# A hybrid transformer block on one core: both seams of its feed-forward rebuilt

## The chip, the cores and the metric

The kernel runs on one core of a Trainium2 chip. The metric is device time in microseconds (us) of one execution, from runs of the kernel before and of the changed one on the same chip. The engines are PE (TensorE, the matrix engine), DVE (VectorE), ACT (ScalarE), POOL (GpSimd) and SP (SyncE, which here only issues DMA transfers). Each runs its own instructions in a fixed order; they wait for each other through semaphores.

## The reference

One residual block on x of 1024 rows (tokens) by 1024 columns: a mixing layer, a cross-attention, and the feed-forward part that the change is about. All in fp32.

```python
D_MODEL, SEQ, D_FF = 1024, 1024, 2816
def reference(x, mem, ...):
    ...
    h = h + jnp.concatenate([ret, fox], axis=-1) @ w_out[l]
    h = h + memory_cross_attention(rmsnorm(h, g_xattn[l]), mem, ...)
    hn = rmsnorm(h, g_ffn[l])
    h = h + (jax.nn.silu(hn @ w_gate[l]) * (hn @ w_up[l])) @ w_down[l]
    return h
```

## The kernel before

**Precision.** PE multiplies fp32 values as pairs: a high part (ACT casts it to a rounded format: `act.copy(hi, x)`) and a low part (DVE: `lo = x - hi`). A product is three matmuls, hi·hi, hi·lo and lo·hi (`into`, L1153 to L1160, per block of 128 in the contraction). So each operand costs an ACT cast and a DVE subtraction before PE can use it.

**Stages.** They run one after the other (`whole`): mixing, cross-attention, its output projection (`xo_main`, which also normalises h for the feed-forward: `f_norm(t)` for the eight row tiles t of 128), the hidden stage (`hidden_main`) and the down stage (`down_main`). The places where the hidden stage starts and ends are the two seams.

**Hidden stage.** The 1024x1024 normalised input is taken as 2x2 blocks x11, x12 (row tiles 0 to 3, tile `xr0`) and x21, x22 (row tiles 4 to 7, `xr1`), and for each of 22 chunks f of 128 hidden columns the weights of gate and up as a second 2x2 matrix. Seven block products in the manner of Strassen and Winograd, P1, Q5, P6, P2, P7, Q3, Q4 (`step`), take the place of eight; each has 12 matmuls of 128x512. On the input side that needs four sums of blocks, s1 = x21 − x22, s3 = x11 − x21, s2 = s1 − x11, s4 = x12 + s2; on the weight side t13 (two sums), t2, t4 per chunk (`weights_of`). P1 and P2 need x11 and x12 alone, so those of the first three chunks run before the first seam (AHEAD = 3). After them, once all eight `f_norm` are done, the four sums and the five split operands are made on whole 128x2048 tiles (L1233 to L1254). Weights come by four loads per chunk into `raw_w` (two buffers, `load_w`), POOL makes the sums, ACT and DVE split them, up to eight products ahead of PE. The result of a chunk, 128x1024, is built in `at` (one buffer) and stored to `a_dram` by SP (L1222).

**Down stage.** Strassen's seven products again, over groups of chunks: GROUPS are four groups of 6, 6, 6 and 4 chunks, each split in two halves along the contraction. Per group eight blocks are loaded (A11 to A22 from `a_dram`, B11 to B22 from w_down; `load`, ten buffers `raw_d`), POOL makes eight combinations into `st` (`combine`), ACT and DVE split 14 operands into `op` tiles (12 buffers), PE runs 7 products x 4 row tiles, and DVE adds each 128x512 result onto the output rows `hh0` to `hh7`, which are loaded from `h_dram` (L1388) and stored to `out` in the last group. Operands are made up to three products ahead.

**Order.** PE's order is written out by hand (`manual_schedule`); on the other engines a scheduler sets it, and a tile's memory may be taken by a later tile once the readers of the first are done, across `pool`s too. So a load can wait for work on quite other data whose memory it takes over. `sp.dma_start` puts a transfer on SP's queue, `pol.dma_start` on POOL's.

Of the kernel before, what the change touches and what calls it, by code (L numbers as in the profile page):

```python
# [1455 lines left out]
```

## Time and profile before

| | us |
|---|---|
| three runs | 1649.39, 1650.70, 1653.69; median 1650.7 |
| profiled execution | 1651.59, of which the span of the core 1649.7 |
| PE busy | 1558.5 (94% of the span) |
| DVE busy | 959.0 (58%) |
| ACT busy | 753.6 (46%) |
| POOL busy | 390.9 (24%) |

Busy time is a sum over the whole span; the stages differ. How to read it: the chain of waits tells which engine's work set the end, a table of stretches tells where that engine stood still or had a lower clock (PEclk, as a share of full speed), and the timeline of such a stretch tells what it waited for, in brackets behind the first instruction after a pause. A row's duration includes a little of the instruction's start and end, so rows of one engine overlap slightly. The end of a matmul in the trace is modelled; the distance from start to start is what counts.

### The profile page before, as it was taken

The numbers are of one execution on the slowest core, as the hardware profiler recorded it, in microseconds if no ns is written. First come the engines' busy times: TensorE is split into PE (matmuls) and PEld (weight loads), VectorE is DVE, ScalarE is ACT, GpSimd is POOL, SyncE is SP. The second block draws the span as 40 slices with busy tenths as digits, with TensorE's granted clock in tenths as the row PEclk, the third lists the DMA queues.
The fourth block names the chain that finished last, engine by engine and source line by source line (L and its number), as shares of the span: only waits on it lengthen the run. The fifth ranks groups of instructions, "written<-read, shape, count | busy, mean of one in ns | idle before, by whom it ended". The sixth has DMA issues, their size and how long they took to land.

```text
span 1649.7 us, 22047 instructions
## 1 busy us (share of the span) xinstructions
PE 1558.5 (94%) x7960; PEld 1313.2 (80%) x7960; DVE 959.0 (58%) x1984; ACT 753.6 (46%) x1630; POOL 390.9 (24%) x387
## 2 busy tenths in 40 slices
PE   7999999999999999999899929999999999589999
PEld 7997898898887878888788817888888887468887
DVE  6667657657668832655644365443444442788877
ACT  5456656656568820555634433333333332323332
POOL 0332232232231000000000033223222220757541
PEclk9999999999999999999999969999999999789999
DMA  7021111121133461202523023222222211833202
GB/s 222 18 75 46 44 52 46 37 60 46 35 114 122 146 205 39 65 14 64 154 83 109 39 76 102 90 77 77 78 90 88 78 51 45 324 123 107 89 15 103
DMA packets 142927, 142.16 MB, mean 86 GB/s; under 512 B 9177, under 2 KB 110809, under 8 KB 142306
## 3 DMA queue, kind: packets, MB, share of 16 engines
q1 hardware_dynamic: 142818, 140.75, 27.1%
q8 instruction: 63, 1.03, 0.3%
q14 instruction: 46, 0.38, 0.1%
HBM read 112.38 MB, written 28.34 MB: 85 GB/s over the span
## 4 chain that ended last, share of the span: by engine, by line
PE 81%; DVE 6%; ACT 5%; DMA 3%; issue 2%; POOL 2%; SPq 0%; POOLq 0%; DVEq 0%; ACTq 0%
PE ps_mm L270 10%; PE ps_mm L271 10%; PE ps_mm L272 10%; PE ps_s L1157 6%; PE ps_s L1158 6%; PE ps_s L1159 6%; PE ps_tp L175 5%; PE ps_tp L1157 3%; PE ps_tp L1159 3%; PE ps_tp L1158 3%; PE ps_mm L1159 2%; PE ps_mm L1158 2%; PE ps_mm L1157 2%; PE ps_s L270 1%; PE ps_pv L696 1%
## 5 line engine op out<-in xcount | busy, mean ns | idle before, releaser
L270 PE MATMUL ps_mm<-w_hi,cv_hi 128*128 128x512 f32 x384 | 155.4, 405 | 6.9 <-DVE h L838 3.5
L272 PE MATMUL ps_mm<-w_hi,cv_lo 128*128 128x512 f32 x384 | 152.1, 396 | 0.0
L271 PE MATMUL ps_mm<-w_lo,cv_hi 128*128 128x512 f32 x384 | 151.7, 395 | 0.0
L1292 ACT CAST w_hi<-t 128x512 fp32r<-128x512 f32 x88 | 54.4, 620 | 171.3 <-PE ps_tp L1158 72.6
L1293 DVE TENSOR_TENSOR w_lo<-t,w_hi 128x512 fp32r<-128x512 f32 x88 | 65.1, 742 | 83.3 <-ACT w_hi L1292 83.2
L1278 POOL TENSOR_TENSOR t<-raw_w 128x1024 f32<-128x1024 f32 x22 | 53.2, 2417 | 250.8 <-DVE w_lo L1293 227.8
L240 DVE TENSOR_TENSOR w_lo<-raw,w_hi 128x1024 fp32r<-128x1024 f32 (+2 forms) x75 | 88.2, 1181 | 30.3 <-ACT w_hi L239 29.3
L239 ACT CAST w_hi<-raw 128x1024 fp32r<-128x1024 f32 (+2 forms) x75 | 74.9, 1003 | 59.2 <-PE ps_mm L272 39.9
L1247 POOL TENSOR_TENSOR xr<-xr,xr 128x2048 f32<-128x2048 f32 x1 | 4.5, 4550 | 396.7 <-DVE s L1245 396.7
L270 PE MATMUL ps_mm<-w_hi,hn_last 128*128 128x384 f32 (+2 forms) x256 | 96.3, 376 | 1.0 <-DVE t L291 1.0
L270 PE MATMUL ps_mm<-w_hi,hn_hi 128*128 128x384 f32 (+2 forms) x256 | 96.4, 377 | 0.1
L271 PE MATMUL ps_mm<-w_lo,hn_hi 128*128 128x384 f32 (+2 forms) x256 | 91.4, 357 | 0.0
L272 PE MATMUL ps_mm<-w_hi,hn_lo 128*128 128x384 f32 (+2 forms) x256 | 91.1, 356 | 0.0
L270 PEld LDWEIGHTS ps_mm<-w_hi,cv_hi 128*128 128x128 f32 x384 | 73.0, 190 | 22.4 <-DVE h L838 4.0
L272 PE MATMUL ps_mm<-w_hi,hn_last 128*128 128x384 f32 (+2 forms) x256 | 90.1, 352 | 0.0
L271 PE MATMUL ps_mm<-w_lo,hn_last 128*128 128x384 f32 (+2 forms) x256 | 89.8, 351 | 0.0
L1337 DVE TENSOR_TENSOR op<-st,op 128x1536 fp32r<-128x1536 f32 (+1 forms) x32 | 79.9, 2530 | 11.8 <-ACT op L1336 11.8
L272 PEld LDWEIGHTS ps_mm<-w_hi,cv_lo 128*128 128x128 f32 x384 | 72.8, 190 | 16.9
L1293 DVE TENSOR_TENSOR w_lo<-raw_w,w_hi 128x512 fp32r<-128x512 f32 x60 | 46.3, 771 | 67.4 <-ACT w_hi L1292 67.4
L271 PEld LDWEIGHTS ps_mm<-w_lo,cv_hi 128*128 128x128 f32 x384 | 73.0, 190 | 14.7
L1336 ACT CAST op<-st 128x1536 fp32r<-128x1536 f32 (+1 forms) x32 | 43.0, 1372 | 86.2 <-POOL st L1332 30.6
L1332 POOL TENSOR_TENSOR st<-raw_d 128x1536 f32<-128x1536 f32 (+1 forms) x16 | 63.9, 4004 | 66.4 <-DMA raw_d<-a_dram 56.7
(394 smaller groups left out, 4577.5 us busy)
## 6 DMA issues: line engine op xcount, KB each, us to landing
raw_w<-w_gate SPq DMA_DIRECT2D x44, 256.0 KB, 3.8
raw_w<-w_up SPq DMA_DIRECT2D x44, 256.0 KB, 4.2
a_dram<-at SPq DMA_DIRECT2D x22, 512.0 KB, 2.6
raw_d<-a_dram SPq DMA_DIRECT2D x12, 768.0 KB, 6.5
raw_d<-w_down SPq DMA_DIRECT2D x12, 768.0 KB, 6.3
raw<-w_in SPq DMA_DIRECT2D x32, 256.0 KB, 4.2
raw<-w_xkv SPq DMA_DIRECT2D x16, 512.0 KB, 3.8
of<-o_dram SPq DMA_DIRECT2D x16, 512.0 KB, 4.1
```

Of the source, the lines that this page charges most:

```text
L175: flip = lambda o, x: mm.transpose(o, x, ident)
L239: act.copy(hi, raw)
L240: dve.tensor_tensor(lo, raw, f32(hi), ALU.subtract)
L270: mm.matmul(o, xh, wh, start=first, stop=False)
L271: mm.matmul(o, xh, wl, start=False, stop=False)
L272: mm.matmul(o, xl, wh, start=False, stop=last)
L1157: mm.matmul(q, wh, xh, start=first and k == 0, stop=False, skip_group_check=True)
L1158: mm.matmul(q, wh, xl, start=False, stop=False, skip_group_check=True)
L1159: mm.matmul(q, wl, xh, start=False, stop=k == n - 1, skip_group_check=True)
L1293: dve.tensor_tensor(lo, x, f32(hi), ALU.subtract)
L1332: pol.tensor_tensor(t, x, y, op)
L1337: dve.tensor_tensor(lo, x, f32(hi), ALU.subtract)
```

## The change

**First seam.** The tiles of h become pairs, so that the first pair can be read as one 128x4x512 tile (`h01`). For t from 4 on, `f_norm` makes the four sums for its 128 rows on DVE, s1 into `h01`, the others in place in `xr`. Behind the seam only the five splits are left, in two slices of columns, 384 and 128. The rows of h are stored to `h_dram` from POOL's queue. The weight tiles `raw_w`, t13, t2 and t4 get a pool of their own (`ra`), and the three weight sums move from POOL to DVE.

**Second seam.** `a_dram` is stored from POOL's queue. The ten `raw_d` buffers are named slots; the first three lie in a pool (`down_r0`) where `ra` was. Three groups of 6, 8 and 8 chunks take the place of four; a buffer holds up to four chunks. The combinations are made on DVE, in place in `raw_d`, and `op` has 10 buffers. Loads are issued as slots come free, up to one group ahead.

```diff
-    GROUPS = [[list(range(f, f + n)), list(range(f + n, f + 2 * n))] for f, n in ((0, 3), (6, 3), (12, 3), (18, 2))]
+    GROUPS = [[list(range(f, f + n)), list(range(f + n, f + 2 * n))] for f, n in ((0, 3), (6, 4), (14, 4))]
...
-        h = [hp.tile([P, D], F32, name=f"h{t}") for t in range(NT)]
-        st["h"] = h
+        pairs = [hp.tile([P, 2, D], F32, name=f"h{t}") for t in range(NT // 2)]
+        st["h"] = [pairs[t // 2][:, t % 2] for t in range(NT)]
+        st["h01"] = pairs[0].rearrange("p a (b c) -> p (a b) c", c=512)
...
-            sp.dma_start(h_dram[t], h[t])
+            pol.dma_start(h_dram[t], h[t])
...
+            if t >= 4:
+                x11, x12, x21, x22 = (st["xr"][i // 2][:, 4 * (i % 2):4 * (i % 2) + 4, cols] for i in range(4))
+                s1 = st["h01"][:, :, cols]
+                dve.tensor_tensor(s1, x21, x22, ALU.subtract)
+                dve.tensor_tensor(x21, x11, x21, ALU.subtract)
+                dve.tensor_tensor(x11, s1, x11, ALU.subtract)
+                dve.tensor_tensor(x12, x12, x11, ALU.add)
...
-                            sp.dma_start(a_dram[g][i][fs.index(f)], c)
+                            pol.dma_start(a_dram[g][i][fs.index(f)], c)
...
-        s12 = pool("ffn_s", 1, stack=tmp).tile([P, 4, 512], F32, name="s12")
-        dve.tensor_tensor(s12, x21, x22, ALU.subtract)
-        A["Q5"] = operand("s1", s12)
-        pol.tensor_tensor(x21, x11, x21, ALU.subtract)
...
+        xs = {"Q5": st["h01"], "P6": xr[0][:, :4], "P7": xr[1][:, :4], "Q3": xr[0][:, 4:], "Q4": xr[1][:, 4:]}
+        for what, x in xs.items():
+            A[what] = [wp[0].tile([P, 4, 512], F32R, name=f"x{what}{i}") for i in range(2)]
+        for cols in (slice(0, 384), slice(384, 512)):
+            for what, x in xs.items():
+                hi, lo = (y[:, :, cols] for y in A[what])
+                act.copy(hi, x[:, :, cols])
+                dve.tensor_tensor(lo, x[:, :, cols], f32(hi), ALU.subtract)
...
+        ra = pool("ffn_a", 1, side="right", stack=RR)
...
-            raw[f] = r = rr.tile([P, 4, 4, P], F32, name="raw_w", tag="raw_w", bufs=2)
+            raw[f] = r = ra.tile([P, 4, 4, P], F32, name="raw_w", tag="raw_w", bufs=2)
...
-                pol.tensor_tensor(t13[f], r[:, 0:2], r[:, 1:3], ALU.add)
+                dve.tensor_tensor(t13[f], r[:, 0:2], r[:, 1:3], ALU.add)
...
-            x = dr.tile([P, 3, 512], F32, name="raw_d", tag="raw_d", bufs=10)[:, :len(fs)]
+            i = room.pop(0)
+            x = dr[i // 3 > 0].tile([P, 4, 512], F32, name="raw_d", tag=f"raw_d{i}")[:, :len(fs)]
...
-            pol.tensor_tensor(t, x, y, op)
...
+            elif what == "Q5":
+                sub(a11, a11, a21)
+                sub(a21, a21, a22)
+                add(b11, b11, b12)
+                x, y = a21, b11
+            elif what == "P6":
+                dve.scalar_tensor_tensor(a21, a11, -1.0, a22, ALU.mult, ALU.subtract)
+                add(b11, b11, b22)
+                x, y = a21, b11
...
+            while todo and room and todo[0][0] <= g + 1:
+                load(*todo.pop(0))
```

DVE's order at the first seam, before (`xr_10132` is `xr0` with x11 and x12, `xr_10133` is `xr1` with x21 and x22, `s_10759` the buffer of s1 and s2):

```order
L1190 TENSOR_TENSOR p_10693<-ps_mm,p_10693 128x512
L1245 TENSOR_TENSOR s_10759<-xr_10133 128x2048
L1190 TENSOR_TENSOR p_10734<-ps_mm,p_10734 128x512
L1239 TENSOR_TENSOR s1l<-s_10759,s1h 128x2048
L1239 TENSOR_TENSOR s3l<-xr_10133,s3h 128x2048
L1248 TENSOR_TENSOR s_10759<-s_10759,xr_10132 128x2048
L1239 TENSOR_TENSOR x22l<-xr_10133,x22h 128x2048
L1239 TENSOR_TENSOR s2l<-s_10759,s2h 128x2048
L1250 TENSOR_TENSOR xr_10132<-xr_10132,s_10759 128x2048
L1239 TENSOR_TENSOR s4l<-xr_10132,s4h 128x2048
L1293 TENSOR_TENSOR w_lo<-t_10803,w_hi 128x512
```

and now (`xr_10126` and `xr_10127` are `xr0` and `xr1`, `h_7710` the pair `h01`, `t_10817` the weight sum t13; L1200 is the addition behind P2):

```order
L1125 TENSOR_TENSOR h_7710<-xr_10127 128x4x128
L1126 TENSOR_TENSOR xr_10127<-xr_10126,xr_10127 128x4x128
L1127 TENSOR_TENSOR xr_10126<-h_7710,xr_10126 128x4x128
L1128 TENSOR_TENSOR xr_10126<-xr_10126 128x4x128
L1200 TENSOR_TENSOR p_10744<-ps_mm,p_10744 128x512
L1251 TENSOR_TENSOR xQ_10767<-h_7710,xQ_10766 128x4x384
L1251 TENSOR_TENSOR xP_10769<-xr_10126,xP_10768 128x4x384
L1251 TENSOR_TENSOR xP_10771<-xr_10127,xP_10770 128x4x384
L1251 TENSOR_TENSOR xQ_10773<-xr_10126,xQ_10772 128x4x384
L1251 TENSOR_TENSOR xQ_10775<-xr_10127,xQ_10774 128x4x384
L1251 TENSOR_TENSOR xQ_10767<-h_7710,xQ_10766 128x4x128
L1251 TENSOR_TENSOR xP_10769<-xr_10126,xP_10768 128x4x128
```

The sums stand ahead of the last P2's addition (L1200) now, the low parts (L1251) behind it in slices, and the first weight sum, which was POOL's, follows them on DVE after five of 128 columns.

SP's queue at the second seam, before:

```order
L1222 DMA a_dram_1_74<-at 128x1024
L1325 DMA raw_d<-a_dram_0_67 128x3x512
L1222 DMA a_dram_1_74<-at 128x1024
L1327 DMA raw_d<-w_down 128x3x512
L1325 DMA raw_d<-a_dram_0_67 128x3x512
L1325 DMA raw_d<-a_dram_1_68 128x3x512
L1327 DMA raw_d<-w_down 128x3x512 x2
L1325 DMA raw_d<-a_dram_1_68 128x3x512
L1327 DMA raw_d<-w_down 128x3x512
L1325 DMA raw_d<-a_dram_0_69 128x3x512
L1327 DMA raw_d<-w_down 128x3x512
L1388 DMA hh_13876<-h_dram 128x1024
```

and now:

```order
L1270 DMA raw_w<-w_gate 128x4x128
L1325 DMA raw_d<-a_dram_0_67 128x3x512
L1327 DMA raw_d<-w_down 128x3x512
L1325 DMA raw_d<-a_dram_0_67 128x3x512
L1385 DMA hh_13891<-h_dram 128x1024
L1385 DMA hh_13893<-h_dram 128x1024
L1385 DMA hh_13895<-h_dram 128x1024
L1325 DMA raw_d<-a_dram_1_68 128x3x512
L1327 DMA raw_d<-w_down 128x3x512 x2
L1325 DMA raw_d<-a_dram_1_68 128x3x512
L1327 DMA raw_d<-w_down 128x3x512
```

The store of `a_dram` is no longer on this queue; A11, B11 and A21 come right behind the last weights, three of the `hh` loads follow, and the fourth load (A22, `a_dram_1_68`) heads the rest.

DVE's order at the second seam, before (`st` are POOL's combinations, `op` the split operands):

```order
L1218 TENSOR_TENSOR at<-at,s_13802 128x512
L1337 TENSOR_TENSOR op_13841<-raw_d,op_13840 128x1536
L1337 TENSOR_TENSOR op_13845<-raw_d,op_13844 128x1536
L1337 TENSOR_TENSOR op_13853<-st,op_13852 128x1536
L1337 TENSOR_TENSOR op_13857<-st,op_13856 128x1536
L1337 TENSOR_TENSOR op_13869<-st,op_13868 128x1536
L1337 TENSOR_TENSOR op_13873<-st,op_13872 128x1536
L1337 TENSOR_TENSOR op_13935<-st,op_13934 128x1536
L1337 TENSOR_TENSOR op_13939<-raw_d,op_13938 128x1536
L1400 TENSOR_TENSOR hh_13876<-hh_13876,ps_s 128x512
```

and now:

```order
L1228 TENSOR_TENSOR at<-at,s_13816 128x512
L1333 TENSOR_TENSOR op_13859<-raw_d,op_13858 128x1536
L1333 TENSOR_TENSOR op_13863<-raw_d,op_13862 128x1536
L1343 TENSOR_TENSOR raw_d<-raw_d 128x1536
L1397 TENSOR_TENSOR hh_13891<-hh_13891,ps_s 128x512
L1343 TENSOR_TENSOR raw_d<-raw_d 128x1536
L1397 TENSOR_TENSOR hh_13893<-hh_13893,ps_s 128x512
L1342 TENSOR_TENSOR raw_d<-raw_d 128x1536
L1333 TENSOR_TENSOR op_13874<-raw_d,op_13873 128x1536
L1333 TENSOR_TENSOR op_13878<-raw_d,op_13877 128x1536
L1353 SCALAR_TENSOR_TENSOR raw_d<-raw_d 128x1536
L1342 TENSOR_TENSOR raw_d<-raw_d 128x1536
```

The combinations (L1342, L1343, L1353) stand in DVE's order between the low parts, and two of the output rows (L1397) stand ahead of the sums that need A22 and B12.

## Rows read from the trace of the kernel before

**Rows 1.** the page's part 4, shares of the chain of waits by engine.

```profile
PE 81%; DVE 6%; ACT 5%; DMA 3%; issue 2%; POOL 2%; SPq 0%; POOLq 0%; DVEq 0%; ACTq 0%
```

**Rows 2.** stretches: us, busy us by engine, PEclk, DMA share, GB/s.

```profile
900.00:949.30 49.30, 49.24 (x230) 40.17 (x228) 18.79 (x32) 18.34 (x32) 1.67 (x1) 1.00 0.09 33
949.30:988.00 38.70, 7.69 (x25) 5.42 (x25) 24.73 (x16) 13.39 (x16) 12.31 (x7) 0.65 0.30 82
988.00:1050.00 62.00, 61.07 (x253) 48.71 (x254) 32.42 (x42) 21.24 (x38) 22.39 (x13) 0.97 0.31 95
1050.00:1401.00 351.00, 351.00 (x1500) 282.15 (x1498) 137.73 (x205) 118.26 (x205) 84.89 (x48) 1.00 0.24 74
1401.00:1457.00 56.00, 30.94 (x93) 22.45 (x92) 43.16 (x15) 15.14 (x11) 43.90 (x10) 0.73 0.77 281
1520.00:1649.70 129.70, 126.06 (x557) 104.04 (x555) 102.93 (x104) 37.78 (x31) 50.93 (x15) 1.00 0.21 72
```

**Rows 3.** timeline, PE: start, us, line, op, out<-in, count, [idle <-releaser].

```profile
978.27 0.80 PE L1157 MATMUL ps_tp<-s1h,w_hi 128*128 128x512 f32 x1 [29.04 <-ACT w_hi L1292]
...
982.93 0.40 PE L1157 MATMUL ps_s<-s2h,w_hi 128*128 128x512 f32 x1
...
987.92 0.50 PE L1157 MATMUL ps_tp<-s4h,w_hi 128*128 128x512 f32 x1 [2.02 <-ACT q L1197]
```

**Rows 4.** timeline, DVE, first seam.

```profile
945.26 2.29 DVE L1245 TENSOR_TENSOR s<-xr 128x2048 f32<-128x2048 f32 x1 [1.66 <-ACT xr L1113]
...
949.95 4.38 DVE L1239 TENSOR_TENSOR s1l<-s,s1h 128x2048 fp32r<-128x2048 f32 x1
...
954.25 2.28 DVE L1239 TENSOR_TENSOR s3l<-xr,s3h 128x2048 fp32r<-128x2048 f32 x1
...
967.30 2.29 DVE L1239 TENSOR_TENSOR s4l<-xr,s4h 128x2048 fp32r<-128x2048 f32 x1 [1.96 <-ACT s4h L1238]
```

**Rows 5.** timeline, ACT, SP's queue and POOL, first seam.

```profile
944.17 1.06 ACT L1113 COPY xr<-ps_tp 128x512 f32<-128x512 f32 x2
...
969.74 0.38 SPq L1272 DMA_DIRECT2D raw_w<-w_gate  x1
...
975.23 2.34 POOL L1278 TENSOR_TENSOR t<-raw_w 128x1024 f32<-128x1024 f32 x1 [23.05 <-DMA raw_w<-w_up]
...
977.60 0.62 ACT L1292 CAST w_hi<-t 128x512 fp32r<-128x512 f32 x1 [10.33 <-POOL t L1278]
```

**Rows 6.** timeline, PE, second seam.

```profile
1410.03 0.80 PE L1157 MATMUL ps_s<-op,op 128*128 128x512 f32 x1 [8.68 <-ACT op L1336]
...
1421.55 0.50 PE L1157 MATMUL ps_mm<-op,op 128*128 128x512 f32 x1
...
1426.55 0.80 PE L1158 MATMUL ps_mm<-op,op 128*128 128x512 f32 x1 [4.50 <-DVE op L1337]
...
1446.97 0.77 PE L1157 MATMUL ps_s<-op,op 128*128 128x512 f32 x1 [9.52 <-DVE hh L1400]
```

**Rows 7.** timeline, SP's queue, DVE, ACT and POOL, second seam.

```profile
1402.80 0.32 SPq L1222 DMA_DIRECT2D a_dram<-at  x1
...
1403.44 1.76 DVE L1337 TENSOR_TENSOR op<-raw_d,op 128x1536 fp32r<-128x1536 f32 x1 [0.67 <-ACT op L1336]
...
1408.51 1.47 ACT L1336 CAST op<-raw_d 128x1536 fp32r<-128x1536 f32 x1 [5.10 <-DMA raw_d<-w_down]
...
1413.03 6.95 POOL L1332 TENSOR_TENSOR st<-raw_d 128x1536 f32<-128x1536 f32 x2 [56.71 <-DMA raw_d<-a_dram]
...
1414.18 12.37 SPq L1388 DMA_DIRECT2D hh<-h_dram  x8
...
1441.26 4.97 DVE L1337 TENSOR_TENSOR op<-raw_d,op 128x1536 fp32r<-128x1536 f32 x1
```

**Rows 8.** groups by form, DVE, 1050 to 1649: busy us, mean ns | idle.

```profile
L1400 DVE TENSOR_TENSOR hh<-hh,ps_s 128x512 f32<-128x512 f32 x42 | 27.2, 679 | 4.2 <-PE ps_s L1159 4.2
```

**Rows 9.** the page's part 6, DMA issues: count, KB each, median us to landing.

```profile
a_dram<-at SPq DMA_DIRECT2D x22, 512.0 KB, 2.6
```

More of the change, by code (lines that the diff above doesn't have):

```diff
@@ L1314, in down_main @@
         dl = pool("down_l", 1)
-        dr = pool("down_r", 1, side="right")
-        raw, tmp = {}, {}
+        dr = [pool(f"down_r{i}", 1, side="right") for i in range(2)]
+        BLOCKS = ("A11", "B11", "A21", "A22", "B12", "B22", "A12", "B21")
+        raw = {}
+        room = list(range(10))
         def load(g, name):
@@ L1338, in split @@
             return hi, lo
-        LOADS = {"P1": ("A11", "B11"), "Q5": ("A21", "A22", "B12"), "P6": ("B22",), "Q3": ("A12",), "P2": ("B21",)}
         PRODUCTS = ("P1", "Q5", "P6", "Q3", "P7", "P2", "Q4")
+        todo = [(g, x) for g in range(len(GROUPS)) for x in BLOCKS]
         def operands(g, what):
-            r = lambda name: raw[g, name]
-            t = lambda name: tmp[g, name]
+            a11, b11, a21, a22, b12, b22, a12, b21 = (raw[g, x][0] for x in BLOCKS)
+            add = lambda o, x, y: dve.tensor_tensor(o, x, y, ALU.add)
+            sub = lambda o, x, y: dve.tensor_tensor(o, x, y, ALU.subtract)
@@ L1356, in operands @@
-            if what == "Q3":
-                combine(g, "S4", r("A12"), t("S2"), ALU.add)
-                return split(t("S4")) + split(r("B22"))
-            if what == "P7":
-                combine(g, "S3", r("A11"), r("A21"), ALU.subtract)
-                combine(g, "T3", r("B12"), r("B22"), ALU.add)
-                return split(t("S3")) + split(t("T3"))
-            if what == "P2":
-                return split(r("A12")) + split(r("B21"))
-            combine(g, "T4", t("T2"), r("B21"), ALU.add)
@@ L1366, in operands @@
-            return split(r("A22")) + split(t("T4"))
+                x, y = a11, b11
+            elif what == "Q5":
[7 more added lines that the diff above has]
+                x, y = a21, b11
+            elif what == "Q3":
+                add(a21, a21, a12)
+                x, y = a21, b22
+            elif what == "P7":
+                add(b12, b12, b22)
+                x, y = a11, b12
+            elif what == "P2":
+                x, y = a12, b21
+            else:
+                add(b11, b11, b21)
+                x, y = a22, b11
@@ L1368, in down_main @@
+            made = split(x) + split(y)
+            for name in {"Q3": ("A21",), "P7": ("A11", "B12", "B22"), "P2": ("A12",), "Q4": ("B21", "A22", "B11")}.get(what, ()):
+                room.append(raw[g, name][1])
+            while todo and room and todo[0][0] <= g + 1:
+                load(*todo.pop(0))
+            return made
         banks = [[ps_s(), ps_s(), ps_s(), ps_pv()], [ps_mm(), ps_mm()] + [ps_tp().rearrange("p a b -> p (a b)") for _ in range(2)]]
         seq = [(g, p) for g in range(len(GROUPS)) for p in PRODUCTS]
-        loads = [(g, x) for g, p in seq for x in LOADS.get(p, ())]
@@ L1371, in down_main @@
-        for x in loads[:8]:
-            load(*x)
-        loaded = 8
+        for _ in BLOCKS:
+            load(*todo.pop(0))
         made = []
@@ L1376, in down_main @@
             while len(made) < min(n + 3, len(seq)):
[L1377 to L1384 removed]
+                made.append(operands(*seq[len(made)]))
             if n == 0:
```

49 lines of the change are left out of this document (8 added, 41 removed).

## The prediction

> **What bounds the kernel now.** I read the page's chain of waits first, then a table of stretches, then the timeline of the two stretches in which the matrix engine is not full. The chain belongs to PE for 81% [rows 1], so only time that PE stands still, or runs at its lower clock, can be won. The table [rows 2] shows where that is: from 900 to 949.3 us PE is busy 49.24 of 49.30, from 1050 to 1401 all of 351.00. The holes are 949.3 to 988 (7.69 of 38.70, granted clock 0.65) with some remainder up to 1050, and 1401 to 1457 (30.94 of 56.00, granted clock 0.73). A matmul of the hidden stage takes 351.00/1500 = 0.234 us, of the down stage 126.06/557 = 0.2263. So the first seam loses 38.70 + 62.00 − (25 + 253) × 0.234 = 35.6 us, the second 56.00 − 93 × 0.2263 = 35.0 us. These 70.6 us are all that the change can touch; it leaves the number of matmuls (924 in the down stage either way) as it was.
>
> In the first seam PE waits 29.04 us for the first w_hi [rows 3]. The chain behind it: DVE makes the sums and low parts from 945.26 one after the other, until 967.30 + 2.29 = 969.6 [rows 4]; only then does SP issue the first raw_w load (969.74), because its buffer lies where the operands' inputs were; POOL starts the sum of weights when it has landed (975.23), ACT casts at 977.60 [rows 5]. The matmuls then start at half speed: Q5's twelve take 982.93 − 978.27 = 4.66 us, where 12 × 0.234 = 2.81, and another 2.02 us wait follows for ACT's copy q [rows 3].
>
> In the second seam PE waits 8.68 us for ACT's cast of B11 [rows 6], which came by a load that SP issues right behind the stage's last store (1402.80 + 0.32, so at about 1403.2), 5.3 us before the cast at 1408.51 [rows 7]. Then 4.50 us for a low part and 9.52 us for DVE's output rows [rows 6]: POOL makes the combinations one after another from 1413.03, and DVE runs beside it at 4.97 us for a tile that took 1.76 alone [rows 7].
>
> **First seam, part by part.** The four sums move ahead of the seam: per row tile t from 4 to 7, four DVE operations of 128x4x128, each about a 128x512 one, 0.68 us [rows 8]; taken at 0.60 where they follow each other (a row's end lies 0.08 behind the next one's start: 949.95 + 4.38 against 954.25 [rows 4]). 16 × 0.60 = 9.6 us go into a stretch where DVE is busy 18.79 of 49.30 [rows 2]: hidden, and at PE's cost only if DVE lacked 20 us more there. The last tile's copies end at 944.17 + 1.06 = 945.23 [rows 5], so its sums are done at 945.26 + 4 × 0.60 = 947.7, before PE's last matmul ends (978.27 − 29.04 = 949.23).
>
> What is left behind the seam: ten casts on ACT, and ten low parts on DVE (five of 1536 columns, five of 512). ACT starts at about 947.0 and needs 5 × 1.40 + 5 × 0.52 = 9.6 us; it stays ahead. DVE is free after the last P2 eviction at 949.95, where s1l starts before [rows 4]. The five large ones at 1.67 (1.76 less the overlap [rows 7]) end at 958.3, the small ones at 0.60 at 961.3. The sum of weights t13, now on DVE (1024 columns, 2 × 0.60 less one overhead, 1.13), ends at 962.4; ACT's cast of 0.62 [rows 5] lets PE start at about 963.15. Loads of raw_w now wait for h stores only, long landed, so they cover themselves; without that cover they would add 5.5 us (969.74 to 975.23).
>
> PE starts 978.27 − 963.15 = 15.1 us earlier. The 2.02 wait, and the half-clock stretch behind it, go as well: by my order of ACT, q is copied at 970.0 and P6 ends at 963.15 + 4.66 + 2.81 = 970.6. Lost after: 963.15 − 949.23 = 13.9, and 4.66 − 2.81 = 1.85 for the clock; 15.75 in place of 35.6. **Gain 19.9 us.** POOL's sums of weights go to DVE in the hidden stage too: 22 chunks × (1.13 + 0.60 + 0.60) = 2.3 us per chunk, where DVE is busy 137.73 of 351 us, 7.7 per chunk of 19.7 [rows 2]. 10.0 of 19.7 stays hidden; in return DVE's low parts no longer run beside POOL.
>
> **Second seam.** A11, B11 and A21 now have places that come free before the end, so their loads leave the path. ACT casts A11 at about 1401.95 (its silu comes first) and B11 right behind it, 2 × 1.45, so PE starts at 1404.85: 3.5 us of idle time after 1401.35 (1410.03 − 8.68). P1 took 1421.55 − 1410.03 = 11.5 us for 36 matmuls [rows 6], half clock and a short wait included; I keep that, 3.35 over 36 × 0.2263. It ends at 1416.35.
>
> The next operands hang on A22: its slot lies where `at` was, so its load waits for the last store of `at`, and SP holds everything behind it (B12, B22, A12, B21, two loads of the next group, hh3 to hh7). That store moves to POOL's queue; from SP it took 2.6 us in the median of 22 [rows 9], an estimate of 3.0 for this end. No row shows a DMA of POOL's queue with this data, so I bound it: 2.6 below, 12.4 above (all eight hh loads of the same 512 KB leave within 12.37 us [rows 7], so no single one can well take longer); nothing below 2.6, since the bytes are the same. I take 3.0, since nothing crowds it. Issue 1402.80, landed 1405.8, A22 there 5.3 later, 1411.1. DVE in its order: low parts of A11 and B11 (1403.44 as before, then to 1406.8), a11−a21 to 1408.45, hh0's row, a21−a22 from 1411.1 to 1412.8, hh1's row to 1413.4, b11+b12 to 1415.1, two low parts to 1418.45. PE's third matmul of Q5 would come at 1416.35 + 0.45: a wait of 1.65 us. Each us that the store takes longer adds about one. The rest follows without a gap by the same count: P6's operands after two sums and two low parts more, 4 × 1.67, at 1425.1 (Q5 ends at 1426.2); Q3's after two rows, two sums and two low parts, 7.9 us, at 1433.0 (P6 ends at 1434.4). From there PE's work, 8.2 us a product, outlasts DVE's.
>
> Lost after: 3.5 + 3.35 + 1.65 = 8.5 in place of 35.0. **Gain 26.5 us**, or 25 if the short wait lowers the clock once more. The sums on DVE cost 8 tiles a group where POOL had them; DVE then needs by its rows some 53.5 of PE's 57.1 us in the group of 6 and 65.7 of 76.2 in those of 8, against 102.93 of 126 in the table's last stretch [rows 2]. The larger groups save output rows (28 fewer at 0.68), already in those figures.
>
> **Sum.** 19.9 + 26.5 = 46.4 us. The profiled execution took 1651.6, so 1605.2; it lies 0.9 over the median of the runs, 1650.7, so I forecast **1604 us**.
>
> **Rivals.** *The store on POOL's queue is late.* For it: [rows 4] and [rows 7] show that POOL and DVE hold each other up (4.38 against 2.29, 4.97 against 1.76), and right behind the last store's issue DVE runs two-input work without a break from 1403.44 to 1408.45. If POOL gets to it only then, A22 comes 5.7 us later: 1610; at the bound of 12.4 us, 9.4 later: 1614. The Trainium skill, page "SBUF — State Buffer", section "SBUF: two separate sides", speaks for it: a DMA issued from POOL has its descriptors written by that engine, which DVE in a two-port mode locks out. No run here shows yet whether fp32 additions do that to a DMA.
>
> *DVE held by late output rows.* The 9.52 us wait of before was of this kind [rows 6]. hh3 comes behind 6.0 MB on SP's queue, in all 6.55 MB. At the 339 GB/s of the eight hh loads (4.19 MB in 12.37 us [rows 7]) it lands at 1405.8 + 19.3 and some 2 us of start, 1427, where DVE wants it at 1429.0 and PE has 1.4 us to spare; at the 281 of the table [rows 2] it comes at 1431, and PE waits 0.7; at 200 it comes at 1440.6, and PE waits 10: 1614.
>
> *The cadence changes.* 0.234 in one stage and 0.2263 in the other for the same shape of matmul isn't explained by a row. If new places in SBUF give the hidden stage the lower one, 1500 × 0.0077 = 11.5 less, 1592; if the down stage gets the higher one, 924 × 0.0077 = 7 more, 1611.
>
> *The first seam doesn't come early.* If the loads of raw_w still left only when DVE is done, the diff would not do what it says; 5.5 us for landing and the late start of casts would leave 1604 + 9 to + 15, up to 1619. The order of loads and their buffers speak against it.
>
> *Slower.* `at` has one buffer; its next write comes about five products (5 × 2.81 = 14 us) after the store's issue. In the hidden stage a store that takes 14 + x us delays each of 19 chunks by x. From x = 46.4/19 = 2.4, a latency of 16.4 us, the whole gain is spent; at 18 us the kernel takes 1604 + 19 × 4 = 1680. That lies beyond the bound of 12.4; only DVE's hold on POOL could make it so, and DVE is idle half the time there, so it is unlikely.
>
> **How the numbers follow.** Forecast, 1598 to 1609: 0.58. Late store: 0.14. Late output rows: 0.09. Cadence: 0.08 (half each way). First seam late: 0.05. Slower by the stores: 0.04, with 0.02 for a smaller latency that eats just the gain. That leaves faster by over 0.3% (about what a measurement can tell) 0.94, within it 0.02, slower 0.04. The range from 1594 to 1618 leaves out the lower cadence, the slower case and the upper end of the first seam.
>
> **What would show it.** Right: PE's first Q5 matmul about 963 instead of 978, no wait for q; in the down stage a first matmul 3.5 us after the last hidden one, one wait of 1 to 3 us before Q5 and none of more than 1 us behind it; DVE tiles of 1536 columns at 1.76 throughout. Wrong: the A22 load issued later than 5 us after the stage's end, waits of PE for DVE in the groups of 8, or another spacing of matmuls in 1050 to 1401.

## The result and the profile after

| | before | after |
|---|---|---|
| median of the runs compared | 1652.2 us (1649.4 to 1655.5) | 1608.4 us (1603.95 to 1609.57) |
| ratio, 95% interval | | 0.973 (0.970 to 0.976) |
| profiled execution, its span | 1651.6, 1649.7 | 1609.22, 1607.5 |
| span: start to end of the last P2 | 949.23 | 950.39 (+1.2) |
| last P2 to end of the hidden stage | 452.12 | 433.17 (−18.9; forecast −19.9) |
| hidden stage's end to end of span | 248.35 | 223.94 (−24.4; forecast −26.5) |

The change made the kernel 2.7% faster, inside the forecast's range and 4.4 us above the 1604 that it names. By the medians the gain is 43.8 us, where the forecast's sum has 46.4.

The table of stretches of the changed kernel answers to [rows 2] (us, then busy us and count of PE, PEld, DVE, ACT, POOL, then granted clock, DMA share, GB/s):

```profile
900.00:949.30 49.30, 49.30 (x231) 40.55 (x230) 27.24 (x48) 18.70 (x34) 1.59 (x3) 1.00 0.27 86
949.30:988.00 38.70, 24.66 (x94) 19.34 (x93) 34.86 (x44) 21.05 (x33) 0.53 (x1) 0.78 0.30 87
...
1040.00:1380.00 340.00, 340.00 (x1453) 273.34 (x1452) 170.75 (x246) 115.27 (x199) 9.04 (x17) 1.00 0.26 80
1380.00:1440.00 60.00, 53.26 (x221) 42.58 (x220) 52.19 (x46) 22.49 (x16) 0.53 (x1) 0.94 0.84 304
1440.00:1500.00 60.00, 60.00 (x266) 49.71 (x265) 58.36 (x45) 22.52 (x12) 0.00 (x0) 1.00 0.30 104
1500.00:1607.50 107.50, 103.36 (x456) 85.23 (x455) 77.80 (x64) 28.18 (x15) 0.00 (x0) 0.99 0.13 50
```

PE now works 24.66 of the 38.70 us behind the first seam (7.69 before), and 53.26 of 60 at the second. The stretch of 900 to 949.3 took DVE's sums without a loss for PE (49.30 of 49.30). From 1440 to 1500 DVE is busy 58.36 of 60 us, and PE still loses nothing. The spacing of matmuls is what it was: 340.00/1453 = 0.234 and 103.36/456 = 0.2267.

PE's timeline at both seams (start, us, line, tile; in brackets the idle time ahead and what ended it) answers to [rows 3] and [rows 6]:

```profile
964.43 0.79 PE L1167 MATMUL ps_tp<-xQ,w_hi 128*128 128x512 f32 x1 [14.04 <-ACT w_hi L1290]
...
970.83 0.40 PE L1167 MATMUL ps_s<-xP,w_hi 128*128 128x512 f32 x1
...
1387.04 0.80 PE L1167 MATMUL ps_s<-op,op 128*128 128x512 f32 x1 [3.48 <-ACT op L1332]
1389.13 0.79 PE L1168 MATMUL ps_s<-op,op 128*128 128x512 f32 x1 [1.30 <-DVE op L1333]
...
1393.94 0.39 PE L1167 MATMUL ps_s<-op,op 128*128 128x512 f32 x1
...
1400.19 0.50 PE L1167 MATMUL ps_mm<-op,op 128*128 128x512 f32 x1 [0.64 <-ACT op L1332]
1402.02 0.50 PE L1168 MATMUL ps_mm<-op,op 128*128 128x512 f32 x1 [1.33 <-DVE op L1333]
```

These five waits are all that is left of 0.5 us or more from 900 on; where [rows 6] has 8.68, 4.50 and 9.52 there are now 3.48, 1.30, 0.64 and 1.33. DVE and ACT of the same kernel, against [rows 4, 5, 7]:

```profile
951.11 1.75 DVE L1251 TENSOR_TENSOR xQ<-h,xQ 128x1536 fp32r<-128x1536 f32 x1
...
962.46 1.22 DVE L1276 TENSOR_TENSOR t<-raw_w 128x1024 f32<-128x1024 f32 x1
...
1389.00 1.75 DVE L1343 TENSOR_TENSOR raw_d<-raw_d 128x1536 f32<-128x1536 f32 x1
...
1394.61 1.76 DVE L1343 TENSOR_TENSOR raw_d<-raw_d 128x1536 f32<-128x1536 f32 x1 [0.96 <-DMA raw_d<-a_dram]
...
948.14 1.48 ACT L1250 CAST xQ<-h 128x1536 fp32r<-128x1536 f32 x1
...
963.76 1.35 ACT L1290 CAST w_hi<-t 128x512 fp32r<-128x512 f32 x2 [5.53 <-DVE t L1276]
```

What bounds the first seam is now DVE's row of low parts from 951.11 and the sum of weights behind it (962.46); ACT, which cast from 948.14, waits 5.53 us for it. DVE tiles of 1536 columns take 1.75 everywhere, where POOL beside them had made one 4.97 [rows 7]. The queues of SP and POOL (issue time):

```profile
898.65 0.67 SPq L1270 DMA_DIRECT2D raw_w<-w_gate  x1
...
1380.79 1.29 SPq L1385 DMA_DIRECT2D hh<-h_dram  x3
1388.81 0.37 SPq L1325 DMA_DIRECT2D raw_d<-a_dram  x1
...
1385.28 0.53 POOL L1232 DMA_DIRECT2D a_dram<-at  x1 [19.15 <-DVE at L1228]
```

The first raw_w leaves at 898.65 instead of 969.74 [rows 5]. The last store leaves POOL at 1385.28, the load of A22 behind it at 1388.81: 3.5 us. That is 5.25 us behind the hidden stage's end (1387.04 − 3.48 = 1383.56).

### The profile page after: what moved, and what is told of

Read it like the earlier page. It is cut to its first block, busy times and chain, and to the rows that moved or that the text cites. A ratio compares the mean times of both kernels' runs of the same rounds, so it can differ in the third digit from the quotient of the medians.

```text
span 1607.5 us, 21839 instructions
## 1 busy us (share of the span) xinstructions
PE 1552.7 (97%) x7960; PEld 1311.5 (82%) x7960; DVE 995.0 (62%) x2050; ACT 751.8 (47%) x1621; POOL 155.2 (10%) x318
## 4 chain that ended last, share of the span: by engine, by line
PE 85%; DVE 5%; ACT 5%; DMA 2%; issue 2%; POOL 1%; SPq 0%; POOLq 0%; DVEq 0%; ACTq 0%
PE ps_mm L270 10%; PE ps_mm L271 10%; PE ps_mm L272 10%; PE ps_s L1167 7%; PE ps_s L1169 7%; PE ps_s L1168 7%; PE ps_tp L175 5%; PE ps_tp L1167 4%; PE ps_tp L1168 4%; PE ps_tp L1169 4%; PE ps_mm L1168 2%; PE ps_mm L1169 2%; PE ps_mm L1167 2%; PE ps_pv L696 1%; PE ps_s L270 1%
## 5 line engine op out<-in xcount | busy, mean ns | idle before, releaser
L1332 ACT CAST op<-raw_d 128x2048 fp32r<-128x2048 f32 (+1 forms) x42 | 72.7, 1764 | 126.5 <-issue 50.8
L1291 DVE TENSOR_TENSOR w_lo<-t,w_hi 128x512 fp32r<-128x512 f32 x88 | 60.3, 687 | 65.8 <-ACT w_hi L1290 65.8
L1333 DVE TENSOR_TENSOR op<-raw_d,op 128x2048 fp32r<-128x2048 f32 (+1 forms) x42 | 87.3, 2109 | 8.1 <-ACT op L1332 8.1
L1167 PE MATMUL ps_tp<-xQ,w_hi 128*128 128x512 f32 x176 | 70.8, 402 | 14.0 <-ACT w_hi L1290 14.0
L1290 ACT CAST w_hi<-raw_w 128x512 fp32r<-128x512 f32 x60 | 37.2, 621 | 89.5 <-PE ps_s L1168 85.6
L1168 PE MATMUL ps_tp<-xQ,w_hi 128*128 128x512 f32 x176 | 70.9, 403 | 0.0
L1169 PE MATMUL ps_tp<-xQ,w_lo 128*128 128x512 f32 x176 | 70.7, 402 | 0.0
```

The costliest lines, as they stand in the source:

```text
L1167: mm.matmul(q, wh, xh, start=first and k == 0, stop=False, skip_group_check=True)
L1168: mm.matmul(q, wh, xl, start=False, stop=False, skip_group_check=True)
L1169: mm.matmul(q, wl, xh, start=False, stop=k == n - 1, skip_group_check=True)
L1333: dve.tensor_tensor(lo, x, f32(hi), ALU.subtract)
```

## The experiments

Each kernel is timed against the kernel before on the same chip, whose median there was 1651.4 to 1654.0. So kernels are compared by their gain, the difference of the two medians: the changed kernel's is 43.8 us (1652.2 to 1608.4). The intervals of the ratios reach 0.0015 to 0.0028 to either side, 2.4 to 4.6 us of 1650, so two gains less than some 4 us apart are not told apart by the times alone; there the text says what the traces add. Each trace is of one execution: in the kernels that leave the part ahead of the first seam as changed, the last P2 ends between 947.0 and 952.5 us.

**Are the seams independent?** The first seam of the change, with the old down stage, old groups and stores on SP:

```diff
-    ... for f, n in ((0, 3), (6, 4), (14, 4))]
+    ... for f, n in ((0, 3), (6, 3), (12, 3), (18, 2))]
...
-                            pol.dma_start(a_dram[g][i][fs.index(f)], c)
+                            sp.dma_start(a_dram[g][i][fs.index(f)], c)
...
-    (down_main of the changed kernel)
+    (down_main of the kernel before)
```

> The kernel before with the first seam of the change alone; the down stage, its four groups and the a_dram stores on SP's queue are as before. Theory (each seam's gain is its own path, and the two add up): the first Q5 matmul starts 14 us after the last P2 one, as in the changed kernel, and the second seam loses its 35 us as before; 18 to 19 us less than before, about 1633 us. Rival (the gains depend on each other, say because the second seam's loads profit from the new places of the first): the difference is not 18 to 19 us; under 15 or over 23.

Measured 1634.2, ratio 0.989 (0.986 to 0.991): a gain of 19.8, the forecast's term for this seam. PE waits 14.04 at 961.29, and at the second seam the old waits are back (the large ones 10.63, 4.11, 10.66, 2.62), 30.0 us in all where the kernel before has 25.1. That leaves 24.0 of the 43.8 to the second seam, about what the span shows there (24.4): within what the times can tell, the terms add. Only one direction is tested. No kernel has the second seam alone, and the kernel with late weights below shows that the second seam leans on a pool of the first.

**What each piece of the first seam is worth.** First the four sums as whole tiles again, behind the last copy, but still on DVE:

```diff
-                dve.tensor_tensor(s1, x21, x22, ALU.subtract)
...
+        dve.tensor_tensor(xs1, x21, x22, ALU.subtract)
+        dve.tensor_tensor(x21, x11, x21, ALU.subtract)
+        dve.tensor_tensor(x11, xs1, x11, ALU.subtract)
+        dve.tensor_tensor(x12, x12, x11, ALU.add)
```

> The changed kernel with the four input sums made behind the tiles' last copy as whole 128x2048 operations on DVE, as before, and everything else as changed. Theory (what counts is how much DVE work stands between the last copy and the first weight): 4 x 2.2 us of sums come back onto the path, less what fits ahead of the last P2 addition; PE starts 6 to 9 us later than in the changed kernel, 1614 to 1618 us. Rival (the early loads of raw_w made the gain of the first seam, the sums didn't): no more than 2 us, 1608 to 1611 us.

```profile
968.18 0.80 PE L1158 MATMUL ps_tp<-xQ,w_hi 128*128 128x512 f32 x1 [18.89 <-ACT w_hi L1287]
```

Measured 1614.0, ratio 0.976 (0.974 to 0.978): a gain of 40.0, 3.8 less than the change, between the two expectations. The two intervals overlap; the trace decides. PE waits 4.85 us longer, though the first raw_w leaves as early as in the changed kernel (897.55), and two of the four sums stand behind the last P2's addition on DVE (950.45 and 954.32, 2.28 each). So DVE, not a load, holds this seam, and the sums come off its row there by being made per tile.

Then the places of the weights' loads back into the pool that opens late:

```diff
-        ra = pool("ffn_a", 1, side="right", stack=RR)
...
-            raw[f] = r = ra.tile([P, 4, 4, P], F32, name="raw_w", tag="raw_w", bufs=2)
+            raw[f] = r = rr.tile([P, 4, 4, P], F32, name="raw_w", tag="raw_w", bufs=2)
```

(likewise t13, t2 and t4).

> The changed kernel without the pool of their own for raw_w, t13, t2 and t4: they lie in the pool of the split weights, where the operands' inputs were, so the first loads wait for DVE's last low part. Theory: the first load leaves at about 962 instead of before 915, lands 5.3 us later, and PE starts about 5.5 us later, at 970; 1613 to 1615 us. Rival (the loads hide behind other work on the path anyway): no difference, 1607 to 1610 us.

SP's queue, then PE:

```profile
961.35 0.37 SPq L1269 DMA_DIRECT2D raw_w<-w_gate  x1
...
1386.92 0.37 SPq L1326 DMA_DIRECT2D raw_d<-w_down  x1
...
1402.96 9.13 SPq L1384 DMA_DIRECT2D hh<-h_dram  x7
...
1393.84 0.79 PE L1167 MATMUL ps_s<-op,op 128*128 128x512 f32 x1 [6.95 <-ACT op L1331]
...
1420.67 0.47 PE L1167 MATMUL ps_s<-op,op 128*128 128x512 f32 x1 [2.61 <-DVE hh L1396]
```

Measured 1620.1, ratio 0.980 (0.978 to 0.982): a gain of 33.9, 9.9 less. At the first seam PE waits 19.35 instead of 14.04, 5.3 more, where the prediction priced the cover at 5.5. That is about half of it: the pool `ra` is also the place of the down stage's first loads, so B11 (the 1386.92 row) comes late, and the second seam waits 6.95 instead of 3.48, and 2.61 for an output row. From the hidden stage's end this trace takes 231.2 us, the changed kernel 223.9. The expectation had not seen that one buffer serves both seams.

Last, the sums of weights on POOL:

```diff
-                dve.tensor_tensor(t13[f], r[:, 0:2], r[:, 1:3], ALU.add)
+                pol.tensor_tensor(t13[f], r[:, 0:2], r[:, 1:3], ALU.add)
```

(and the two that follow it).

> The changed kernel with the three weight sums t13, t2 and t4 on POOL again; input sums, buffers and loads as changed. Theory (the sum t13 on DVE stands on the path, and its loads have long landed): POOL makes t13 ahead of the seam and PE starts 1 to 4 us earlier; behind that POOL's later sums slow DVE's tiles beside them and give up to 3 us of it back; 1605 to 1609 us. Rival (POOL beside DVE costs more than it saves at this seam, as in the kernel before): 3 to 8 us slower, over 1611 us.

```profile
962.50 0.79 PE L1167 MATMUL ps_tp<-xQ,w_hi 128*128 128x512 f32 x1 [12.30 <-ACT w_hi L1290]
...
981.69 0.50 PE L1167 MATMUL ps_s<-xQ,w_hi 128*128 128x512 f32 x1 [2.47 <-DVE at L1217]
```

Measured 1609.8, ratio 0.974 (0.972 to 0.976): a gain of 43.8, no difference. PE starts 1.74 earlier and pays 2.47 some 19 us later for a DVE operation. That piece of the change is neutral.

**Which engine makes the combinations.** Seven of the eight sums of the down stage on POOL, its operand pools as changed:

```diff
-            add = lambda o, x, y: dve.tensor_tensor(o, x, y, ALU.add)
-            sub = lambda o, x, y: dve.tensor_tensor(o, x, y, ALU.subtract)
+            add = lambda o, x, y: pol.tensor_tensor(o, x, y, ALU.add)
+            sub = lambda o, x, y: pol.tensor_tensor(o, x, y, ALU.subtract)
```

> The changed kernel with seven of the eight combinations of a group in the down stage on POOL, in place as in the changed kernel; the scalar_tensor_tensor stays on DVE. The early loads stay. Theory (at the second seam the combinations on POOL, and DVE slowed beside them, made about half of the loss, the late loads the rest): PE waits again before Q5, P6 and Q3, in sum 10 to 18 us with the half clock behind the waits; 1619 to 1626 us. Rival (the early loads and buffers made nearly all of the second seam's gain): under 5 us, 1608 to 1613 us.

POOL, DVE and PE of this kernel:

```profile
1389.33 4.75 POOL L1343 TENSOR_TENSOR raw_d<-raw_d 128x1536 f32<-128x1536 f32 x1 [1.82 <-DVE op L1333]
...
1396.99 3.50 POOL L1343 TENSOR_TENSOR raw_d<-raw_d 128x1536 f32<-128x1536 f32 x1 [2.91 <-PE ps_s L1169]
...
1402.02 3.47 DVE L1333 TENSOR_TENSOR op<-raw_d,op 128x1536 fp32r<-128x1536 f32 x1 [4.35 <-ACT op L1332]
...
1412.12 0.79 PE L1168 MATMUL ps_mm<-op,op 128*128 128x512 f32 x1 [5.89 <-DVE op L1333]
...
1479.63 0.80 PE L1168 MATMUL ps_s<-op,op 128*128 128x512 f32 x1 [5.41 <-DVE op L1333]
```

Measured 1631.7, ratio 0.987 (0.984 to 0.989): a gain of 22.3, 21.5 less, more than expected. A sum takes 3.50 on POOL with DVE almost idle (the 1396.99 row) and 4.75 where DVE's low parts run into it, against 1.75 on DVE; DVE's low part beside POOL takes 3.47 against 1.75. PE's waits behind 1380 grow by 16.9 us in all, also in the groups of 8 (5.41, 2.22). So nearly the whole gain of the second seam needs DVE for the sums.

**The store's queue, A22's place, the groups.** Three parts alone. The store back on SP:

```diff
-                            pol.dma_start(a_dram[g][i][fs.index(f)], c)
+                            sp.dma_start(a_dram[g][i][fs.index(f)], c)
```

> The changed kernel with the stores of a_dram on SP's queue again; the rest is as changed. Theory (the queue that a store is issued from matters only through the store's own time, 3.5 us from POOL at the end of the hidden stage against 2.6 to 3.0 from SP before): the load of A22 leaves up to 0.9 us earlier, PE's wait before Q5 is up to 0.9 us shorter; 1606 to 1609 us, the same within the measurement. Rival (taking the stores off SP's queue made part of the gain, since loads no longer stand behind them): 3 us or more slower, over 1611 us.

```profile
1381.62 0.32 SPq L1232 DMA_DIRECT2D a_dram<-at  x1
...
1384.76 0.37 SPq L1325 DMA_DIRECT2D raw_d<-a_dram  x1
...
1392.10 0.69 DVE L1397 TENSOR_TENSOR hh<-hh,ps_s 128x512 f32<-128x512 f32 x1 [1.85 <-PE ps_s L1169]
...
1398.28 0.49 PE L1167 MATMUL ps_mm<-op,op 128*128 128x512 f32 x1 [2.14 <-ACT op L1332]
```

Measured 1608.1, ratio 0.973 (0.971 to 0.975), a gain of 45.5: the same. A22 follows the store after 3.1 us here, 3.5 with POOL. The queue brings nothing that the times can tell. The shorter wait that was expected did not come: PE waits 2.14 us before Q5 where the changed kernel has 0.64, since on DVE one output row more (1392.10) stands ahead of a21−a22, and from the hidden stage's end this trace is 2.7 us longer (226.6 for 223.9). Next, A22 itself in a place that comes free early (slots handed out in another order than the loads are issued):

```diff
+        for name in ("A11", "B11", "A21", "A12", "B21", "A22", "B12", "B22"):
+            i = room.pop(0)
+            first[name] = i, dr[i // 3 > 0].tile([P, 4, 512], F32, name="raw_d", tag=f"raw_d{i}")
```

> The changed kernel with the places of two buffers swapped in the first group: A22's load gets a place that is free before the last store of at, and A12's and B21's loads the places that wait for it. Order and number of instructions are the same. Theory (PE's waits of 0.64 and 1.33 us before Q5 hang on that store): A22 is there before the first low parts are done, the two waits fall to 0.3 us or less, 1.5 to 2 us gained, 1606 to 1607 us. Rival (the wait is DVE's own work, not the load): both waits stay, 1608 us.

```profile
1381.16 0.37 SPq L1330 DMA_DIRECT2D raw_d<-a_dram  x1
...
1391.92 0.69 DVE L1405 TENSOR_TENSOR hh<-hh,ps_s 128x512 f32<-128x512 f32 x1 [2.21 <-PE ps_s L1169]
1392.53 1.75 DVE L1348 TENSOR_TENSOR raw_d<-raw_d 128x1536 f32<-128x1536 f32 x1
...
1399.99 0.50 PE L1168 MATMUL ps_mm<-op,op 128*128 128x512 f32 x1 [1.32 <-DVE op L1338]
```

Measured 1606.2, ratio 0.972 (0.970 to 0.973): a gain of 47.4, 3.6 more, with intervals that overlap. Each expectation has half: A22 leaves at 1381.16, the 0.64 wait goes, the 1.32 stays. DVE now stands idle 2.21 us ahead of an output row that needs P1's first result, with a21−a22 (1392.53) queued behind it: DVE's row holds what the load no longer does.

The groups of 6, 6, 6 and 4 chunks with all else changed:

> The changed kernel with the four groups of 6, 6, 6 and 4 chunks of before; the number of matmuls is the same, 28 output rows of 0.69 us more on DVE. Theory (PE is the bound in the down stage as long as DVE's work fits under it; DVE needs some 53.5 of 57.1 us per group): 0 to 2 us slower, 1608 to 1610 us. Rival (DVE becomes the bound without the larger groups): PE waits for low parts or rows in each group, 4 to 12 us slower, over 1612 us.

Measured 1607.9, ratio 0.973 (0.972 to 0.975), a gain of 45.7: the same, with no PE wait of 0.5 us or more beyond the changed kernel's. The larger groups bring nothing that can be measured.

**Taking what is left.** On the kernel with A22's early place, the order on ACT and DVE was pinned: P1's casts and low parts ahead of the last chunk's silu and product, the first output row behind Q5's low parts.

```diff
+                for x in splits[:2]:
+                    after_in_queue(st["last3"], x[1])
+                    for later, earlier in zip(st["last"], x):
+                        after_in_queue(later, earlier)
...
+                row = dve.tensor_tensor(o, o, qs[i], op)
+                if n == 0:
+                    after_in_queue(row, splits[3][1])
```

> The changed kernel with A22's buffer swapped as in a22_slot, and the order at the second seam pinned: ACT casts A11 and B11, and DVE makes their low parts, ahead of the last hidden product's silu and of the at row behind Q3; the first output row hh0 stands behind the low parts of Q5. Theory (what is left of the second seam is order alone: the data of P1 landed 20 us before): PE's waits of 3.48 and 1.30 us at the seam and 0.64 and 1.33 us before Q5 go, and the half-clock stretch of ten matmuls (2 us) with them; 8 to 9 us less than the changed kernel, 1599 to 1601 us. Rival (P1 also waits for a place that only the last hidden product frees): at most the waits before Q5 go, 1605 to 1607 us.

```profile
1377.12 4.17 SPq L1401 DMA_DIRECT2D hh<-h_dram  x7
1381.45 0.37 SPq L1334 DMA_DIRECT2D raw_d<-a_dram  x1
...
1392.74 1.76 DVE L1352 TENSOR_TENSOR raw_d<-raw_d 128x1536 f32<-128x1536 f32 x1 [9.15 <-DMA raw_d<-a_dram]
...
1398.01 0.79 PE L1167 MATMUL ps_mm<-op,op 128*128 128x512 f32 x1 [9.95 <-ACT op L1341]
```

Measured 1611.9, ratio 0.975 (0.973 to 0.976): a gain of 41.3, 6.1 less than the kernel it was made from. That theory fell. P1 does start right behind the hidden stage, and 3.48 and 1.30 are gone; but seven hh loads, 3.7 MB, now stand ahead of A22 on SP's queue, where three stood, so A22 is there 11 us after its issue, and PE waits 9.95 for it one product later. So the queue was pinned as well: A22, B22 and B12 ahead of all hh loads, four of them ahead of A12 and B21, and each product's low parts ahead of the previous one's rows.

```diff
+                    ld = sp.dma_start(h[t], h_dram[t])
+                    after_in_queue(ld, st["ld", 0, "B12"], st["ld", 0, "B22"])
+                    if t == 3:
+                        after_in_queue(st["ld", 0, "A12"], ld)
...
-                if n == 0:
-                    after_in_queue(row, splits[3][1])
+                if i == 0 and n + 1 < len(seq):
+                    after_in_queue(row, splits[2 * n + 3][1])
```

> seam2_order with SP's queue pinned as well: the loads of A22, B22 and B12 ahead of all hh loads, hh0 to hh3 ahead of A12 and B21, hh4 to hh7 ahead of the next group; on DVE each product's low parts stand ahead of the rows of the product before it. Theory (in seam2_order the scheduler put seven hh loads, 3.7 MB, ahead of A22 on the queue, and that is the whole 9.95 us wait before Q5): A22 leaves before the last hidden product ends, the wait before Q5 falls to 1 to 3 us; 7 to 9 us less than seam2_order, 1602 to 1605 us, 4 to 6 less than the changed kernel. Rival (the down stage's start is bound by the sum of bytes, 8.6 MB at some 340 GB/s, whatever their order): the wait moves to P6's or Q3's rows, 1608 to 1612 us.

```profile
1380.33 0.37 SPq L1334 DMA_DIRECT2D raw_d<-a_dram  x1
...
1383.55 1.95 SPq L1402 DMA_DIRECT2D hh<-h_dram  x4
...
1385.28 3.54 DVE L1353 TENSOR_TENSOR raw_d<-raw_d 128x1536 f32<-128x1536 f32 x2
...
1392.06 0.50 PE L1167 MATMUL ps_mm<-op,op 128*128 128x512 f32 x1 [0.55 <-ACT op L1342]
1393.88 0.50 PE L1168 MATMUL ps_mm<-op,op 128*128 128x512 f32 x1 [1.32 <-DVE op L1342]
```

Measured 1599.4, ratio 0.968 (0.967 to 0.970): a gain of 52.1, 10.8 more than without the queue's order and 8.3 more than the change, better than expected. The edit changes the queue and the rows' place on DVE at once; the trace puts it down to the queue, since DVE's 9.15 us wait for A22 is gone (the 1385.28 row is a11−a21 and a21−a22 without a pause). Of the second seam 1.9 us of waits are left. They are no longer held by an output row: none stands ahead of Q5's low parts here.

The first seam was ordered too, once together with each of the last two kernels. The order on ACT and DVE is pinned: the splits of the first 384 columns for Q5 and P6 ahead of the last tile's sums, then what else Q5 needs, then the rest. Q5's first weights get a place of their own (4 KB per partition), so that they can be split early. The lines that pin the order are left out here.

```diff
-        for cols in (slice(0, 384), slice(384, 512)):
-            for what, x in xs.items():
+        for what, x in xs.items():
+            for cols in (slice(0, 384), slice(384, 512)):
...
+            if (f, what) == (0, "Q5"):
+                hi, lo = (fw.tile([P, 4, P], F32R, name=f"w0{i}") for i in range(2))
```

> seam2_order, and at the first seam: Q5 of the first chunk gets weights in a place of their own, the splits of the first 384 columns for Q5 and P6 stand ahead of the last tile's sums, then Q5's last 128 columns, t13 and Q5's weights, then the rest. Theory (behind the first seam PE waits for DVE's work, and what can move ahead of the last copies comes off the wait): PE starts Q5 at about 953 instead of 964 and P6 at about 961 instead of 969.7; 7 to 9 us less than seam2_order, 1591 to 1594 us. Rival (DVE's work behind the seam is the same sum and shows up as waits before P6, Q3 and P7): 0 to 3 us less, 1597 to 1600 us.

```profile
949.67 0.80 PE L1168 MATMUL ps_tp<-xQ,w 128*128 128x512 f32 x1 [3.38 <-ACT w L1301]
...
956.87 0.50 PE L1168 MATMUL ps_s<-xP,w_hi 128*128 128x512 f32 x1 [1.72 <-ACT w_hi L1301]
...
959.29 0.80 PE L1170 MATMUL ps_s<-xP,w_lo 128*128 128x512 f32 x1 [1.70 <-DVE w_lo L1301]
```

Measured 1606.9, ratio 0.972 (0.971 to 0.974): 4.9 below the kernel with the second seam's order alone (1611.9, same chip), between the two expectations. PE waits 6.8 us where it waited 14.04, but in three pieces, and behind them 23 matmuls run at the lower clock (granted clock 0.50) instead of 11 in the kernel without it; 12 × 0.2 = 2.4 of the 7.2 go back.

> both_order with the same queue. Theory: the 5 us that both_order gained over seam2_order at the first seam and the 7 to 9 us of the queue add up; 1597 to 1600 us. Rival: as for seam2_queue, 1603 to 1607 us.

Measured **1595.3**, ratio 0.965 (0.964 to 0.967): the best version, with a gain of 56.2, 12.4 more than the change and 4.1 more than with the pinned queue alone, a little better than expected (runs from 1590.8 to 1597.7). It combines the ordered first seam and the pinned queue. Behind its three waits at the first seam (3.38, 2.79 and 1.20) at least 13 matmuls run at the lower clock, 5 in the kernel with the queue alone.

## Why the prediction was right, and where it was off

**First seam, the wait.** Forecast 13.9 us behind the last P2, measured 14.04, ended by the operation that it named (ACT's cast behind DVE's sum of weights), with 2.02 for q gone. The steps hold in the rows: 1.75 per large low part (1.67 from start to start, as forecast), the sum at 1.22 for 1.13. That the sums per tile cost PE nothing, that the loads leave early, and what they would cost without that (5.5 forecast, 5.3 measured) was shown by the kernels that undo each.

**First seam, the clock.** This term was mis-sized. Forecast 1.85; measured (970.83 − 964.43) − 15 × 0.234 = 2.89, since 13 matmuls behind the wait were spaced 0.427 (granted clock 0.50, the 1.2 GHz level), where the trace of before had 4 behind its wait and then 8 more behind the wait for q. That is the 1.0 us by which the seam missed.

**Second seam, PE's start and P1.** Forecast 3.5, measured 3.48. P1 was kept at its old loss of 3.35; it lost 1400.19 − 0.64 − 1387.04 − 36 × 0.2263 = 4.36, again by more matmuls at the lower clock (10 from 1389.73, 7 before) and by 0.3 of its short wait (1.30 for 1.00).

**Second seam, the wait ahead of Q5.** Forecast 1.65, measured 0.64 + 1.33. The store's price, estimated at 3.0, was 3.5, and A22's landing took 5.8 to DVE's start for 5.3. But the reason was only half right. DVE did wait for A22 (0.96 at 1394.61), so a longer store would have cost time, as "Each us that the store takes longer adds about one" says; a shorter one would have given back at most that. With A22 issued 1.4 us ahead of the hidden stage's end, where it was 5.25 behind it, only 0.64 went and 1.32 stayed, behind DVE, which stood idle 2.21 us ahead of an output row. The prediction had listed that row and not seen that it waits for P1. No kernel moves that row alone: where it stands behind Q5's low parts (the pinned queue), P1 starts earlier too and 1.32 is still there, ended by the second of these low parts. One of the prediction's signs of being wrong came, if narrowly: A22's load left 5.25 us after the stage's end, beyond the 5 that it had set. Behind Q5 no wait came, as forecast. Of the 2.1 us that the seam missed, P1 is 1.0 and this wait 0.3; 0.5 lies behind PE's last matmul (4.53 us from its start to the end of the span, 4.03 before), and the remaining 0.3 are not explained.

**Outside the seams.** 1.2 us were lost ahead of the last P2, in a part that the change leaves alone: behind a wait near 818 us 11 matmuls ran at the lower clock, 6 in the trace of before (5 × 0.2 = 1.0 of it). It is no more than what traces of the same code differ by there (947.0 to 952.5).

**The sum.** These are 1.2 + 1.0 + 2.1 us, against the 4.0 by which the profiled execution (1609.2) lies over the sum for it (1605.2); the 0.3 between them are rounding and time outside the span. Some 2.6 of it is the length of stretches at the lower clock (1.0 near 818 us, 1.0 at the first seam, 0.6 in P1), which the forecast took from one trace as if it were fixed. Behind the first seam the kernels here show 5 to 13 such matmuls, so the 4 of that trace were a low draw.

**The rivals.** The late store did not come: DVE ran two-input work from 1385.65 to 1390.75, and POOL's DMA, issued at 1385.28, was done within 3.5 us in the midst of it. Of all 22 stores from POOL the longest took 5.7 us (1000.45; DVE waited 3.16 us for it, PE did not). The section "SBUF: two separate sides" of the Trainium skill's page "SBUF — State Buffer", to which the prediction turned for this rival, says further on that `tensor_tensor` has no two-port mode, so it does not speak for this rival. The trace agrees as far as it goes: the store at 1385.28 landed 3.3 us after its issue beside such work, where the median of the 22 is 2.9. It is one store, and POOL's row for it overlaps DVE's work by 0.16 us only. Late output rows were no fault of the changed kernel, but the 2.61 wait of the kernel with late weights is of that kind: there no hh load left before 1402.96, where the changed kernel sends three at 1380.79. DVE shows no pause ahead of the row that PE waited for (1419.84), so its place in DVE's order counts there too. The cadence stayed. The loads did leave early. The stores' median from POOL (part 6 of the page of the profile: count, KB each, median us to landing) is far from the 16.4 of the slower case:

```profile
a_dram<-at POOLq DMA_DIRECT2D x22, 512.0 KB, 2.9
```

**What of the change does the work.** DVE instead of POOL for the combinations, places that come free early for the loads, and sums per tile. The store's queue, the groups of 8 and DVE for the sums of weights are neutral within what was measured. Not undone alone, and so not priced: the early issue of loads up to a group ahead, the sums in place with fewer `op` buffers, the splits in two slices, and h's stores on POOL.

## What to carry to other kernels

Where two stages meet, price the chain operation by operation from the rows of the engine that holds it; the waits summed in this way came out to 0.4 us and better here (13.9 for 14.04, 3.5 for 3.48, 1.65 for 1.97), while what was carried over from the old trace, the stretch at the lower clock and P1's loss, missed by 1.0 each time. Then look at the *order* on each queue, DMA queues too: a load whose place is free gains nothing behind 3.7 MB that nobody needs yet, and an order pinned on two engines without the queue was slower than none. Splitting one long wait of PE into several short ones gave part of the gain back to the clock (23 matmuls at the lower clock for 11, and at least 13 for 5).

## What the runs showed of the hardware

- The stretch at the lower clock behind a wait is not fixed by the wait: after PE had stood idle for the same 14.04 us, 5 to 13 matmuls were spaced 0.427 us in the kernels here (granted clock 0.50, the 1.2 GHz level), then 0.234 (1.00). At 0.2 us each that alone moves a run by 1.6 us, so from these traces a forecast can only bound it.
- POOL and DVE side by side slow each other for fp32 operations of 1536 columns: 4.75 on POOL, where it takes 3.48 to 3.50 with DVE idle or nearly so, and 3.47 on DVE, where it takes 1.75 alone.
- A DMA issued by POOL costs about what SP's does: 3.5 against 3.1 us to the dependent load at the stage's end, 2.9 against 2.6 in the median of 22 stores (SP's in the kernel before).
- DVE at 97% (58.36 of 60 us) did not hold up PE (60.00 of 60); the kernel makes its operands up to three products ahead.
